# A third activation buffer, a regrouped gate table in DRAM and a later place for two expert pairs in a mixture-of-experts kernel

## The chip, the cores and the metric

The kernel runs on one core of a Trainium2 chip. Its time is the device time of one execution in microseconds (us); three runs gave 2286.55 to 2287.98 us, median 2287.09 us. The profiled execution, from which every row below is taken, was a little longer: 2294.13 us, with a span of 2292.2 us between its first and its last instruction.

The engines are called by short names: PE is the matrix engine, ACT the scalar engine, DVE the vector engine, POOL the GpSimd engine, SP the engine that only issues transfers. A name with a q (SPq, ACTq) means a transfer that the engine issues. Each of the two issuing engines used here, SP and ACT, has a queue of its own (q1 is SP's, q10 is ACT's), and POOL's gathers run on q0. All three are served by the same 16 DMA engines.

## The reference, cut to what matters

Two transformer-like blocks come first; the change does not touch them. Then comes a product-key mixture of experts over 512 tokens, with 16384 experts, each one row of `u_tab` and one row of `v_tab`:

```
def peer(h, wq, subkeys, u_tab, v_tab):          # h: 512 tokens x 1024
    q = (xt @ wq).reshape(T, 8, 2, 128)
    sc = einsum('thpd,hpkd->thpk', q, subkeys)   # 8 heads, two halves, 128 keys each
    vals, ids = top_k(sc, 16)
    cand = vals[:, :, 0, :, None] + vals[:, :, 1, None, :]
    cid  = ids[:, :, 0, :, None] * 128 + ids[:, :, 1, None, :]
    top, pos = top_k(cand, 16)                   # 16 experts per head: 128 per token
    idx = take_along_axis(cid, pos)
    g = softmax(top)
    ...
        u = take(u_tab, ic); a = einsum('chkd,cd->chk', u, xc)
        wgt = gc * gelu(a)
        vv = take(v_tab, ic); out = einsum('chk,chkd->cd', wgt, vv)
```

The result is x plus gate2 times this sum.

## The kernel before, in words

**Two ways through the experts.** The first 128 tokens fetch their chosen rows of u and v with indirect transfers (POOL issues them at L1184, DVE takes the dot products at L1189 and adds the rows at L1203). The other 384 tokens go densely over all 16384 experts, which are cut into 64 pairs of two blocks of 128 experts. A pair needs the activations a = gelu(u h) (128 experts x 2 x 384 tokens), the gate weights g of the same shape (zero where a token did not choose the expert), and the rows of v. Each product is made of three matmuls on a high and a low part.

**What one pair costs on PE.** The activation half is 48 matmuls with 384 columns (`mmps`, L228 to L230, evicted by ACT at L1171), the output half 36 matmuls with 512 columns (`sp`, `tps`, `ob`), which add into six accumulators kept over the whole loop.

**The stages of this part.** After the scores and the choice of experts come the twelve calls of `gates(tb)`, one per block of 32 of the 384 tokens. Each builds the gate weights of its 32 tokens for all 16384 experts in the tile `stg` (ACT evicts it from `sp` at L1352) and writes 2 MB into the DRAM table `gd` (ACT issues this at L1353, right behind the last eviction). Between these calls `act_ahead` makes the activations of pairs 0 to 31 and writes them into `ad` (L1369, ACT's queue). The loop over `order` follows: 32 pairs whose activations are made in the loop (pairs 32 to 63) and 32 whose activations are read from `ad` into the tile `pa` (L1422, SP's queue). Two pairs of the first kind and two of the second take turns; the last four are 62, 63, 30 and 31. Every second pair reads the gate weights of two pairs from `gd` into the tile `pg` (L1427, SP's queue).

**The chain of one pair in the loop.** `vh` is the high part of the rows of v (ACT, L1432) and `vl` the low one (DVE, L1441). DVE multiplies `pa` with `pg` (L1443), ACT rounds the product to `wh` (L1444), DVE makes the rest `wl` (L1445), and the 36 output matmuls follow. `pa` has two buffers, `pg` three; the tile `half` at the end of the kernel shares the buffers of `pa`.

**What sets the order.** A scheduler orders each engine's instructions when the kernel is built, from its own model of time; every engine then runs its list in that order. A tile that is used again waits for the last reader of the buffer. The first tiles of the loop lie in memory that the gates stage used, so they wait for its last transfers as well.

Of the kernel before, what the change touches and what calls it, by code (L numbers as in the profile page):

```python
# [7 lines left out]
F32 = mybir.dt.float32  # L8
# [11 lines left out]
P = 128  # L20
# [117 lines left out]
def body(tc, i, o):  # L138
    nc = tc.nc
    V, A, G, TE, S = nc.vector, nc.scalar, nc.gpsimd, nc.tensor, nc.sync  # L140
    ctx = ExitStack()

    def pool(name, bufs, st=None, **k):
        if "space" not in k:
            k["reuse_waits"] = "tile"
        return (st or ctx).enter_context(tc.tile_pool(name=name, bufs=bufs, **k))
# [11 lines left out]
    dp = pool("dram", 1, space=bass.MemoryType.DRAM)  # L158
# [50 lines left out]
    def load_raw(view, n):  # L209
        r = wraw.tile([P, KD, CW], F32, name="wr", tag="wr")  # L210
        if n == 0:
            r = r.rearrange("p (e k) n -> p e (k n)", e=2)
            S.dma_start(r, view)
            return r
        S.dma_start(r[:, :, :n], view)
        return r
# [10 lines left out]
    def mm3(ps, sh, sl, mh, ml, first, last):  # L227
        TE.matmul(ps, sh, mh, start=first, stop=False)  # L228
        TE.matmul(ps, sh, ml, start=False, stop=False)  # L229
        TE.matmul(ps, sl, mh, start=False, stop=last)  # L230
# [26 lines left out]
    def ada_steps(*mods):  # L257

        ada_run(mods, [load_raw(m.views[m.n][0], CW) for m in mods])
# [880 lines left out]
    TB = 32  # L1140
    ND = T - P
    NTD = ND // P
    NB = ND // TB
# [9 lines left out]
    for t in range(NT):  # L1153
        S.dma_start(xd[t * P:(t + 1) * P, :], x[:, t, :])
    xst.close()
    gd = dp.tile([NB, P, P * TB], F32, name="gd")
    ad = dp.tile([NSP, P, 2 * ND], F32, name="ad")
    gate2 = Rows(aw2[20:24], c2, i["abg2"][5:6])
    idx = gat.tile([P, NH * TK], I32, name="idx")
# [3 lines left out]
    def expert_act(pr, dst, lo_eng=None):  # L1163

        w = load_split(i["u"][pr], CW, lo_eng)
        for e in range(2):
            ps = psm.tile([P, T], F32, name="mmps", tag="mm")
            sl = slice(e * P, (e + 1) * P)
            for k in range(KD):
                mm3(ps[:, :ND], w[0][:, k, sl], w[1][:, k, sl], hT[0][:, k, P:], hT[1][:, k, P:], k == 0, k == KD - 1)  # L1170
            A.activation(dst[:, e, :], ps[:, :ND], AF.Gelu_apprx_tanh)  # L1171
# [40 lines left out]
    def gather_to(goal):  # L1212
        while done[0] < len(work) and done[1] < goal:
            while fetched[0] < len(work) and fetched[1] + work[fetched[0]][0] - done[1] <= NBUF[0]:
                for f in work[fetched[0]][1]:
                    fetch(*f)
                fetched[1] += work[fetched[0]][0]
                fetched[0] += 1
            n, _, fn, args = work[done[0]]
            fn(*args)  # L1220
            done[0] += 1
            done[1] += n
# [105 lines left out]
    def gates(tb):  # L1328

        stg = rw.tile([P, P, TB], F32, name="stg", tag="stg")  # L1330
        for q8 in range(TB // 8):
            t0 = tb * TB + 8 * q8
            bc = lambda a_: a_[:, t0:t0 + 8].unsqueeze(2).to_broadcast([P, 8, P // 2, 2])
            pairs = lambda z: z.rearrange("p t (k s) -> p t k s", s=2)
            oh = [rw.tile([P, 8, P], F16, name="oh" + n, tag="oh" + n) for n in "pohl"]
            p_, o_, qh, ql = oh
            V.tensor_tensor(pairs(p_), pairs(io16), bc(i0T), op=ALU.is_equal)
            V.tensor_tensor(pairs(o_), pairs(io16), bc(i1T), op=ALU.is_equal)
            q = V.tensor_tensor(pairs(qh), pairs(o_), bc(ghT), op=ALU.mult)
            if q8 % 2:  # L1340
                V.tensor_tensor(pairs(ql), pairs(o_), bc(glT2), op=ALU.mult)
            else:
                for n in range(8):
                    A.activation(ql[:, n, :], o_[:, n, :], AF.Copy, scale=glT[:, t0 + n:t0 + n + 1])
            for q4 in range(2):
                ps = pss.tile([P, 4, P], F32, name="sp", tag="sp")
                for n in range(4):
                    j = 4 * q4 + n
                    TE.matmul(ps[:, n, :], qh[:, j, :], p_[:, j, :], start=True, stop=False)
                    TE.matmul(ps[:, n, :], ql[:, j, :], p_[:, j, :], start=False, stop=True)  # L1350
                tl = 8 * q8 + 4 * q4
                A.activation(stg[:, :, tl:tl + 4], ps.rearrange("p t i -> p i t"), AF.Copy, scale=1.0 / 1024)  # L1352
        A.dma_start(gd[tb], stg.rearrange("p i t -> p (i t)"))  # L1353
        with tc.issue_after(q.ins):
            gather_to(max(0, min(tb, 8) - 4) * 3)

# [2 lines left out]
    def act_ahead(n):  # L1359
        for _ in range(n):  # L1360
            pr = ahead[0]
            if pr >= NSP:
                return
            ahead[0] += 1
            if gate2.n < 4:
                ada_steps(gate2)
            a_ = rw.tile([P, 2, ND], F32, name="aout", tag="aout")
            expert_act(pr, a_)
            A.dma_start(ad[pr], a_.rearrange("p a b -> p (a b)"))  # L1369
# [5 lines left out]
    for t in range(NT):  # L1375
        route(t)
        act_ahead(1)
        if t:
            for tb in range(P // TB):
                gates((t - 1) * (P // TB) + tb)  # L1380
                act_ahead(2)
    act_ahead(NSP)
    rt.close()

# [2 lines left out]
    pp = pool("peer", 2)  # L1387
    pa = pool("peeracc", 1)
# [16 lines left out]
    def x_rows(t):  # L1405
        xr = new_rows()
        S.dma_start(xr, xd[t * P:(t + 1) * P, :])
        return xr

    def half_out(t, s_, xr, ps, eng):  # L1410

        sl = slice(s_ * 512, s_ * 512 + 512)
        z = pp.tile([P, 512], F32, name="half", tag="pa")
        V.tensor_mul(z, ps, gate2.out[:, sl])
        eng.tensor_tensor(xr[:, sl], xr[:, sl], z, op=ALU.add)
        S.dma_start(o["out"][t * P:(t + 1) * P, sl], xr[:, sl])

    for step, pr in enumerate(order):
        end = step == len(order) - 1
        a_ = pp.tile([P, 2, ND], F32, name="pa", tag="pa")  # L1420
        if pr < NSP:
            S.dma_start(a_.rearrange("p a b -> p (a b)"), ad[pr])  # L1422
        else:
            expert_act(pr, a_)
        if pr % 2 == 0:
            g4 = pp.tile([P, NB, 4, TB], F32, name="pg", tag="pg", bufs=3)
            S.dma_start(g4.rearrange("p b i t -> p b (i t)"), gd[:, :, 2 * pr * TB:(2 * pr + 4) * TB].rearrange("b p n -> p b n"))  # L1427
        g_ = g4[:, :, 2 * (pr % 2):2 * (pr % 2) + 2, :]
        vr = load_raw(i["v"][2 * pr * P:(2 * pr + 2) * P].rearrange("(e p) d -> p e d", e=2), 0)
        vh = pp.tile([P, 2, D], F32R, name="vh", tag="vh")  # L1430
        vl = pp.tile([P, 2, D], F32R, name="vl", tag="vl")
        A.activation(vh, vr, AF.Copy)  # L1432
        wh = pp.tile([P, 2, ND], F32R, name="wh", tag="wh")
        wl = pp.tile([P, 2, ND], F32R, name="wl", tag="wl")
        pace = []

        def paced(q):
            pace.append(q)
            with tc.issue_after(q.ins):
                gather_to(early + (total - early) * (sum(cost[:step]) + len(pace) / 3 * cost[step]) / fin)  # L1440
        paced(V.tensor_sub(vl, vr, vh.bitcast(F32)))  # L1441
        av = a_.rearrange("p e (b t) -> p e b t", t=TB)
        paced(V.tensor_tensor(av, av, g_.rearrange("p b e t -> p e b t"), op=ALU.mult))  # L1443
        A.activation(wh, a_, AF.Copy)  # L1444
        paced(V.tensor_sub(wl, a_, wh.bitcast(F32)))  # L1445
        if end:
            gather_to(2 * total)
            xrs = [x_rows(t) for t in range(NT)]
            for s_ in range(2):
                half_out(0, s_, xrs[0], acc[:, s_ * 512:s_ * 512 + 512], G)  # L1450
        for t in range(NTD):
            tsl = slice(t * P, (t + 1) * P)
            for s_ in range(2):
                dsl = slice(s_ * 512, s_ * 512 + 512)
                for e in range(2):
                    mm3(sums[2 * t + s_], wh[:, e, tsl], wl[:, e, tsl], vh[:, e, dsl], vl[:, e, dsl], step == 0 and e == 0, end and e == 1)
                if end:
                    half_out(t + 1, s_, xrs[t + 1], sums[2 * t + s_], G if t == 0 and s_ == 0 else V)
# [19 lines left out]
```

## Time and profile before

| | us |
|---|---|
| median of three runs | 2287.09 |
| the profiled execution | 2294.13 |
| its span | 2292.2 |
| blocks 1 and 2 | up to about 1000 |
| scores, choice of experts | about 1000 to 1295 |
| gates: first and last write of `gd` issued | 1302.1, 1478.4 |
| loop over the pairs | about 1487 to 2285 |
| last result issued | 2289.2 |

PE is busy for 96% of the span, DVE for 75%, ACT for 43%, POOL for 26%. The mean over the span hides stages: in most 50-us stretches PE is busy all the time, and there nothing that another engine does moves the end. What can be lost or gained lies where PE's busy time falls short of the stretch, and each place of that kind has a row in the list of waits. A matmul's mean duration in a row is longer than its pitch, because matmuls overlap; the pitch is read from the starts in the timeline. The granted clock (column PEclk, 1.00 is 2.4 GHz, 0.50 is 1.2 GHz) tells whether the matmuls of a stretch ran at full pitch.

### The profile page before, as it was taken

Reading aid. Unit: us, or ns where it says so; the run is one execution under the profiler, and the core shown is the slowest. Engines: PE = TensorE matmul, PEld = TensorE weight load, DVE = VectorE, ACT = ScalarE, POOL = GpSimd, SP = SyncE. Lnnn points to the kernel's source line nnn. Section 1 sums busy time; section 2 is a strip of 40 time slices with the busy share of each in tenths; the row PEclk is TensorE's granted clock in tenths of the full one; section 3 lists DMA queues with packets and bytes.
Section 4 is the critical chain, followed back from the end, with each engine's and each line's share of the span. In section 5 each row is a group of like instructions: output and inputs, shape, how many; then the busy total and the mean of one; then the engine's idle time right before and its main releaser. Section 6 shows DMA issues by size and latency. Waiting matters only on the chain.

```text
span 2292.2 us, 33232 instructions
## 1 busy us (share of the span) xinstructions
PE 2204.9 (96%) x12667; PEld 1901.6 (83%) x12667; DVE 1726.5 (75%) x3497; ACT 984.0 (43%) x1751; POOL 586.5 (26%) x385
## 2 busy tenths in 40 slices
PE   7999999999999989998999999989999999999998
PEld 4777776987789878697899999878888888888887
DVE  6675788488754478658899998687877778778785
ACT  3335565444433353544334677723333323333331
POOL 1231100210101441010000002155545545435451
PEclk9989999999999899999999999999999999999999
DMA  7531120145432124024345468899989999999993
GB/s 292 207 137 49 38 74 19 65 160 185 158 112 90 38 75 158 19 103 146 127 153 204 180 266 329 310 376 342 333 324 353 336 336 347 333 337 359 332 340 138
DMA packets 151823, 474.38 MB, mean 207 GB/s; under 512 B 14320, under 2 KB 66416, under 8 KB 128624
## 3 DMA queue, kind: packets, MB, share of 16 engines
q1 hardware_dynamic: 108464, 300.28, 36.9%
q0 software_dynamic: 36864, 134.23, 15.6%
q10 hardware_dynamic: 6336, 37.75, 4.2%
q8 instruction: 99, 1.62, 0.3%
q14 instruction: 60, 0.49, 0.1%
HBM read 429.76 MB, written 41.94 MB: 206 GB/s over the span
## 4 chain that ended last, share of the span: by engine, by line
PE 82%; DVE 7%; DMA 5%; ACT 2%; issue 2%; POOL 1%; SPq 0%; ACTq 0%; DVEq 0%; POOLq 0%
PE mmps L228 14%; PE mmps L230 14%; PE mmps L229 14%; PE sp L228 4%; PE sp L229 4%; PE sp L230 4%; PE tps L228 3%; PE sp L490 3%; PE tps L229 2%; PE tps L230 2%; PE tps L514 2%; PE ob L738 2%; DVE adacc L269 2%; DMA pa<-ad 1%; DMA wr<-in_aw_dram 1%
## 5 line engine op out<-in xcount | busy, mean ns | idle before, releaser
L228 PE MATMUL mmps<-hTh,whi 128*128 128x384 f32 (+1 forms) x1624 | 588.8, 364 | 6.1 <-ACT pa L1171 2.5
L229 PE MATMUL mmps<-hTl,whi 128*128 128x384 f32 (+1 forms) x1624 | 584.0, 360 | 1.7 <-DVE hTl L346 1.7
L230 PE MATMUL mmps<-hTh,wlo 128*128 128x384 f32 (+1 forms) x1624 | 582.6, 359 | 2.2 <-DVE wlo L224 2.2
L1184 POOL DMA_INDIRECT rows<-in_un_dram,idx x128 | 211.3, 1651 | 593.7 <-DVE rows L1189 333.6
L228 PEld LDWEIGHTS mmps<-hTh,whi 128*128 128x128 f32 x1624 | 306.6, 189 | 37.8 <-ACT pa L1171 3.7
L230 PEld LDWEIGHTS mmps<-hTh,wlo 128*128 128x128 f32 x1624 | 306.6, 189 | 30.1 <-DVE wlo L224 3.0
L229 PEld LDWEIGHTS mmps<-hTl,whi 128*128 128x128 f32 x1624 | 307.0, 189 | 29.0 <-DVE hTl L346 3.3
L223 ACT ACTIVATE whi<-wr 128x2048 fp32r<-128x2048 f32 x121 | 230.2, 1903 | 154.6 <-PE mmps L229 97.2
L224 DVE TENSOR_TENSOR wlo<-wr,whi 128x2048 fp32r<-128x2048 f32 x111 | 253.1, 2280 | 32.9 <-ACT whi L223 32.3
L1184 POOL DMA_INDIRECT rows<-in_v_dram,idx x128 | 198.4, 1550 | 211.4 <-DVE acc L1203 171.1
L1441 DVE TENSOR_TENSOR vl<-wr,vh 128x2048 fp32r<-128x2048 f32 x64 | 146.5, 2289 | 119.2 <-ACT vh L1432 106.7
L1432 ACT ACTIVATE vh<-wr 128x2048 fp32r<-128x2048 f32 x64 | 122.4, 1914 | 264.4 <-PE ob L230 223.1
L1203 DVE SCALAR_TENSOR_TENSOR acc<-rows,dots,acc 128x1024 f32<-128x1024 f32 x127 | 162.6, 1280 | 1.8 <-DMA rows<-in_v_dram,idx 0.2
L269 DVE SCALAR_TENSOR_TENSOR adacc<-wr,c_c,adacc 128x256 f32<-128x256 f32 x308 | 161.3, 541 | 3.2
L1189 DVE SCALAR_TENSOR_TENSOR rows<-rows,hn 128x1024 f32<-128x1024 f32 x128 | 153.2, 1218 | 10.8 <-DMA rows<-in_un_dram,idx 9.8
L228 PE MATMUL sp<-vh,wh 128*128 128x512 f32 x384 | 145.6, 396 | 13.2 <-ACT wh L1444 13.2
L229 PE MATMUL sp<-vl,wh 128*128 128x512 f32 x384 | 148.7, 395 | 1.5 <-DVE vl L1441 1.5
L230 PE MATMUL sp<-vh,wl 128*128 128x512 f32 x384 | 136.7, 391 | 0.4 <-DVE wl L1445 0.4
L1444 ACT ACTIVATE wh<-pa 128x768 fp32r<-128x768 f32 x64 | 53.2, 842 | 160.6 <-DVE pa L1443 90.8
L228 PE MATMUL mmps<-whi,hTh 128*128 128x256 f32 x336 | 106.6, 318 | 4.2 <-ACT whi L223 2.9
L229 PE MATMUL mmps<-wlo,hTh 128*128 128x256 f32 x336 | 103.9, 310 | 0.6 <-DVE wlo L224 0.6
L230 PE MATMUL mmps<-whi,hTl 128*128 128x256 f32 x336 | 102.5, 311 | 1.1 <-DVE hTl L346 1.1
(1087 smaller groups left out, 4351.0 us busy)
## 6 DMA issues: line engine op xcount, KB each, us to landing
wr<-in_u_dram SPq DMA_DIRECT2D x64, 1024.0 KB
wr<-in_v_dram SPq DMA_DIRECT2D x64, 1024.0 KB
wr<-in_aw_dram SPq DMA_DIRECT2D x48, 1024.0 KB
gd<-stg ACTq DMA_DIRECT2D x12, 2048.0 KB
pg<-gd SPq DMA_DIRECT2D x32, 768.0 KB
wr<-in_dilw_dram SPq DMA_DIRECT2D x16, 1024.0 KB
ad<-aout ACTq DMA_DIRECT2D x32, 384.0 KB
pa<-ad SPq DMA_DIRECT2D x32, 384.0 KB
```

What stands on the lines that cost most here:

```text
L223: A.activation(hi[:, :, :n], r[:, :, :n], AF.Copy)
L224: (lo_eng or V).tensor_tensor(lo[:, :, :n], r[:, :, :n], hi[:, :, :n].bitcast(F32), op=ALU.subtract)
L228: TE.matmul(ps, sh, mh, start=first, stop=False)
L229: TE.matmul(ps, sh, ml, start=False, stop=False)
L230: TE.matmul(ps, sl, mh, start=False, stop=last)
L269: V.scalar_tensor_tensor(acc, r[:, k, :], m.ccol[:, k:k + 1], acc, op0=ALU.mult, op1=ALU.add)
L490: TE.matmul(sp[j], q, k, start=False, stop=True, skip_group_check=True)
L1184: G.indirect_dma_start(out=r, out_offset=None, in_=table, in_offset=bass.IndirectOffsetOnAxis(ap=ix, axis=0))
L1189: V.scalar_tensor_tensor(r, r, 1.0, hn, op0=ALU.mult, op1=ALU.mult, accum_out=dots[:, n:n + 1])
L1203: V.scalar_tensor_tensor(acc, r, dots[:, n:n + 1], acc, op0=ALU.mult, op1=ALU.add)
L1432: A.activation(vh, vr, AF.Copy)
L1441: paced(V.tensor_sub(vl, vr, vh.bitcast(F32)))
```

## The change

It has four edits. The DRAM table `gd` is laid out as [128, 32, 12, 128] in place of [12, 128, 4096]: its second index is a group of four first keys, that is of two pairs, so that what one read takes is contiguous for each partition. The two pairs that `act_ahead` makes less in the first two rounds of the gates are left to the call `act_ahead(NSP)` behind the last gates. The tile `pa` gets a third buffer, `half` with it, and `pg` gives one up.

```
-    gd = dp.tile([NB, P, P * TB], F32, name="gd")
+    gd = dp.tile([P, P // 4, NB, 4 * TB], F32, name="gd")
...
-        A.dma_start(gd[tb], stg.rearrange("p i t -> p (i t)"))
+        A.dma_start(gd[:, :, tb, :], stg.rearrange("p (g i) t -> p g (i t)", i=4))
...
-                act_ahead(2)
+                act_ahead(1 if t == 1 and tb < 2 else 2)
     act_ahead(NSP)
...
-        z = pp.tile([P, 512], F32, name="half", tag="pa")
+        z = pp.tile([P, 512], F32, name="half", tag="pa", bufs=3)
...
-        a_ = pp.tile([P, 2, ND], F32, name="pa", tag="pa")
+        a_ = pp.tile([P, 2, ND], F32, name="pa", tag="pa", bufs=3)
...
-            g4 = pp.tile([P, NB, 4, TB], F32, name="pg", tag="pg", bufs=3)
-            S.dma_start(g4.rearrange("p b i t -> p b (i t)"), gd[:, :, 2 * pr * TB:(2 * pr + 4) * TB].rearrange("b p n -> p b n"))
+            g4 = pp.tile([P, NB, 4, TB], F32, name="pg", tag="pg", bufs=2)
+            S.dma_start(g4.rearrange("p b i t -> p (b i t)"), gd[:, pr // 2].rearrange("p b n -> p (b n)"))
```

**ACT in the gates stage.** The names: `gd<-stg` is the write of gate weights, `ad<-aout` that of activations made ahead. Before:

```order
L1369 DMA ad<-aout 128x768
L1353 DMA gd<-stg 128x4096
L1171 ACTIVATE aout<-mmps 128x384
L1352 ACTIVATE stg<-sp 128x128x4 x3
L1344 ACTIVATE ohl<-oho,glT 128x128 x8
```

After, at the same place:

```order
L1369 DMA ad<-aout 128x768
L1353 DMA gd<-stg 4096x1x128
L1171 ACTIVATE aout<-mmps 128x384
L1352 ACTIVATE stg<-sp 128x128x4 x3
L1344 ACTIVATE ohl<-oho,glT 128x128 x8
```

Nothing moved here; only the write's shape differs, 4096 runs of 128 numbers (512 bytes) where there were 128 runs of 4096 numbers (16 KB). On PE, ACT, DVE and SP the whole list up to the first instructions of the loop holds the same operations in the same order, and all 32 writes of `ad` stand ahead of the last write of `gd`, before and after.

**SP at the start of the loop.** These are the transfers that stand in its queue one behind the other. Before:

```order
L213 DMA wr<-in_v_dram 128x2x1024 x2
L1427 DMA pg<-gd 128x12x128 x3
L213 DMA wr<-in_v_dram 128x2x1024
L215 DMA wr<-in_u_dram 128x2048
L1422 DMA pa<-ad 128x768
L1427 DMA pg<-gd 128x12x128
L1422 DMA pa<-ad 128x768
```

After:

```order
L213 DMA wr<-in_v_dram 128x2x1024 x2
L1427 DMA pg<-gd 128x1536 x2
L213 DMA wr<-in_v_dram 128x2x1024
L1422 DMA pa<-ad 128x768
L215 DMA wr<-in_u_dram 128x2048
L1422 DMA pa<-ad 128x768
L1427 DMA pg<-gd 128x1536
```

Two reads of `pg` stand ahead of the rows of v and not three, the first `pa` stands ahead of the load of u, and a read is 128 runs of 6 KB where it was 1536 runs of 512 bytes.

**PE where the last activations are made.** `mmps_20511` is the second block of pair 63, `wh_20423` and `wh_20542` are the rounded products of pairs 62 and 63. Before:

```order
L229 MATMUL mmps_20511<-hTl_9756,whi_20481 128x384
L230 MATMUL mmps_20511<-hTh_9755,wlo_20482 128x384
L228 MATMUL sp_14928<-vh_20539,wh_20542 128x512
L229 MATMUL sp_14928<-vl_20540,wh_20542 128x512
L228 MATMUL sp_14929<-vh_20539,wh_20542 128x512
```

After:

```order
L229 MATMUL mmps_20511<-hTl_9756,whi_20481 128x384
L230 MATMUL mmps_20511<-hTh_9755,wlo_20482 128x384
L228 MATMUL sp_14928<-vh_20420,wh_20423 128x512
L229 MATMUL sp_14928<-vl_20421,wh_20423 128x512
L228 MATMUL sp_14929<-vh_20420,wh_20423 128x512
```

Before, the output matmuls of pair 63 stand right behind its own last activation; after, the 36 output matmuls of pair 62 stand between the two.

## Rows read from the trace of the kernel before

**Rows 1.** Windows: length, busy us of PE, PEld, DVE, ACT, POOL (instructions), clock, DMA share, GB/s.

```profile
1500.00:1550.00 50.00, 48.60 (x231) 42.01 (x230) 39.34 (x48) 15.92 (x13) 25.01 (x16) 0.99 1.04 391
...
1650.00:1700.00 50.00, 48.26 (x232) 41.76 (x231) 38.90 (x48) 16.16 (x14) 28.32 (x17) 1.00 0.94 341
1700.00:1750.00 50.00, 50.00 (x239) 43.51 (x238) 37.64 (x45) 15.93 (x13) 26.29 (x16) 1.00 0.93 331
```

**Rows 2.** Waits of PE from 1300 to the end: total us, times, longest.

```profile
PE sp L228 <- ACT wh L1444: 13.2, 4, 8.1
```

**Rows 3.** Timeline from the last gate write to the first product, ACT and DVE.

```profile
1478.40 0.33 ACTq L1353 DMA_DIRECT2D gd<-stg  x1
...
1488.97 2.29 DVE L1441 TENSOR_TENSOR vl<-wr,vh 128x2048 fp32r<-128x2048 f32 x1 [12.34 <-DMA gd<-stg]
...
1494.12 0.96 DVE L1443 TENSOR_TENSOR pa<-pa,pg 128x768 f32<-128x768 f32 x1 [0.57 <-DMA pg<-gd]
```

**Rows 4.** Timeline of the loop's end, PE and DVE.

```profile
2255.45 0.34 PE L230 MATMUL mmps<-hTh,wlo 128*128 128x384 f32 x1
...
2257.72 0.95 DVE L1443 TENSOR_TENSOR pa<-pa,pg 128x768 f32<-128x768 f32 x1
...
2259.60 0.80 PE L228 MATMUL sp<-vh,wh 128*128 128x512 f32 x1 [3.82 <-ACT wh L1444]
2260.20 0.63 PE L229 MATMUL sp<-vl,wh 128*128 128x512 f32 x1
2260.62 0.63 PE L228 MATMUL sp<-vh,wh 128*128 128x512 f32 x1
```

**Rows 5.** Matmuls at full clock just before, and windows of 5 us around that gap.

```profile
2252.68 0.39 PE L228 MATMUL ob<-vh,wh 128*128 128x512 f32 x1
2252.91 0.39 PE L229 MATMUL ob<-vl,wh 128*128 128x512 f32 x1
...
2255.00:2260.00 5.00, 1.18 (x6) 0.87 (x5) 4.49 (x4) 2.27 (x4) 0.00 (x0) 0.84 0.00 0
2260.00:2265.00 5.00, 5.00 (x13) 3.85 (x13) 4.29 (x5) 0.28 (x1) 0.00 (x0) 0.50 0.55 184
```

**Rows 6.** Waits of PE between 1500 and 2250.

```profile
PE sp L229 <- DVE vl L1441: 1.5, 1, 1.5
PE mmps L230 <- DVE wlo L224: 1.3, 1, 1.3
PE sp L228 <- ACT wh L1444: 1.2, 2, 1.0
PE mmps L228 <- ACT pa L1171: 0.9, 3, 0.5
```

**Rows 7.** DMA queues from 1302 to 1480, then from 1489 to 1500: packets, MB, share.

```profile
q10 hardware_dynamic: 3744, 28.97, 40.8%
...
q1 hardware_dynamic: 4675, 2.44, 88.2%
```

**Rows 8.** Windows: the gates stage as a whole.

```profile
1302.00:1478.00 176.00, 173.55 (x1447) 164.72 (x1445) 158.07 (x233) 134.42 (x303) 18.91 (x14) 1.00 0.78 297
```

**Rows 9.** Instructions by tile: duration ns min/median/max, first and last start.

```profile
L1353 ACTq DMA_DIRECT2D gd<-stg x12: 326/326/327, 1302.1 to 1478.4; - x12
L1369 ACTq DMA_DIRECT2D ad<-aout x15: 326/326/327, 1310.7 to 1459.6; - x15
L1422 SPq DMA_DIRECT2D pa<-ad x32: 320/338/7836, 1501.6 to 2260.8; - x32
```

**Rows 10.** Timeline of SP where the first gate weights are read.

```profile
1488.92 0.37 SPq L1427 DMA_DIRECT2D pg<-gd  x1
1489.46 0.61 SPq L1427 DMA_DIRECT2D pg<-gd  x1
1490.16 2.73 SPq L1427 DMA_DIRECT2D pg<-gd  x1
```

**Rows 11.** What ended DVE's and ACT's idle time before work on `pa`: us, times.

```profile
  DMA pa<-ad: 23.2, 8
```

## The prediction

> **What bounds the kernel now.** I read the busy shares first, then windows of 50 us, then PE's list of waits, and last the timeline at each place where a wait of PE stands. The windows tell where to look. From 1700 on PE is busy 50.00 of 50 us per window, at full clock, up to the last 50 us: only PE's own work counts there. Between 1500 and 1700 every window falls short, the first by 1.4 and the last by 1.74 us, the four together by 5.1 us [rows 1]. The largest wait by far is that of an output matmul for `wh`, 13.2 us in four times, the longest 8.1 us [rows 2]. It has two homes. One is the passage from the gates to the loop: the last write of `gd` is issued at 1478.40, DVE resumes at 1488.97 when it has landed, and the product at L1443 starts at 1494.12, when the first `pg` has landed [rows 3]. The other is the loop's end: PE makes the last activation at 2255.45, waits 3.82 us for the chain eviction, product, `wh` of that same pair, and runs on from 2259.60 [rows 4].
>
> **The end: -6.4 us.** The order puts the 36 output matmuls of pair 62 between the last activation and the first matmul that needs its `wh`. At full clock such a matmul takes 0.23 us (starts 2252.68 and 2252.91 [rows 5]), so 36 of them cover 8.2 us; the chain to be covered is 2255.45 to 2259.60, 4.15 us [rows 4]. The gap of 3.82 us goes. With it goes what follows it: PE's granted clock is 1.00 before the gap and 0.50 in the 5 us from 2260 (2.4 and 1.2 GHz), with 13 matmuls there [rows 5], which start 0.42 us apart (2260.20, 2260.62 [rows 4]) instead of 0.23: 13 x 0.2 = 2.6 us. What is late next is PE itself. If a load of `pa` for pairs 30 or 31 came late, the same gap would only move; the third buffer lets that load start earlier, so I take the whole 6.4 us, with 0 as the other end.
>
> **Inside the loop: -4 us.** The waits of PE from 1500 to 2250 add up to 4.9 us, of which `wlo` has 1.3 [rows 6]. A third `pa` lets the next pair's activations be evicted and the next `ad` read be issued before the product of the pair before last is used up, and a `pg` read of 8 runs per DMA engine in place of 96 lets what stands behind it in SP's queue start sooner. I take 4 of the 5.1 us missing in the windows [rows 1]; more than 5.1 there is not to be had. Nothing or a loss is possible, since `pg` with two buffers is asked for later and the order is a new one (third rival).
>
> **The gates' last write and first read: +1.9 us.** Prices per megabyte come from the queues. Long runs (8 KB on average): 40.8% of 16 engines for 178 us moved 28.97 MB, 40 engine-us per MB. Runs of 512 bytes: 88.2% of 16 engines for 11 us moved 2.44 MB, 64 engine-us per MB [rows 7]. A write of 2.1 MB thus goes from 5.3 to 8.3 us, +3.1; a read of 0.79 MB from 3.1 to 2.0 us, -1.2. Both lie on the passage's chain one behind the other [rows 3], so +1.9. The ends: -1.2, if a write of 512-byte runs drains as the long one does, and +3.1, if the read gains nothing because its landing is mostly latency. No row shows a write of short runs.
>
> **The other eleven writes: +3 us.** As transfers they lie beside PE's work: PE is busy 173.55 of 176 us in this stage and the DMA engines 0.78 [rows 8]; 12 x 3.1 = 37 us more lift that to 0.99, full but not over. The doubtful part is ACT, which issues them. A write now holds ACT for 0.33 us [rows 9]. After, it has 4096/16 = 256 runs per DMA engine. The nearest rows are SP's three reads in a row, 96 runs per engine each: the first held SP for 0.37 us, the second (192 in all) for 0.61, the third (288) for 2.73 [rows 10]; the three together, 3.97 us, are where 288 leads and 1.1 us where 192 does. In between 256 gives 3.0 us, 2.7 more than now, 12 times: 32 us of ACT's time. ACT has 176 - 134.42 = 41.6 us to spare there [rows 8], so by the sum it is hidden behind PE; but the hold always stands ahead of an eviction, and PE has only two buffers of `mmps` to go on with. I take a tenth of it, 3 us. The ends: -2.4, all of PE's idle time there [rows 8], and +49: a hold as long as the longest of the trace, 7.84 us [rows 9], makes 12 x 7.5 = 90 us against 41.6.
>
> The Trainium skill, Perfetto Trace Analysis, section "DMA Instruction — HWDGE (DVE, Sync)", says that the issuing sequencer stays occupied, with the descriptor generator locked, until all descriptors of its transfer have been generated, and that the descriptor buffer can fill. SP's third read agrees, with its 2.73 us [rows 10]; no row here shows ACT held so. By that rule the sum is the first rival's rather than mine.
>
> **The moved pairs: 0.** The pairs that `act_ahead` leaves out in the first rounds are made at the same place as before: the order up to the loop is unchanged and all writes of `ad` still stand ahead of the last of `gd` (the last now starts at 1459.6 [rows 9]). Their matmuls therefore cover nothing of the passage. So this edit doesn't do what it says, and I count it at nothing.
>
> **The sum.** -6.4 - 4 + 1.9 + 3 = -5.5 us. From the profiled execution, 2294.1, that is 2288.6; this execution stands 7.0 us above the median of the runs, so the forecast is 2287.1 - 5.5 = 2281.6 us. About 0.2%, 4.6 us, is what a measurement of this kernel can tell from no change.
>
> **Rivals.**
> *ACT held until its queue drains (slower).* The new writes share the DMA engines with loads and gathers, so their runs drain more slowly than SP's reads did. Halfway between 3.0 and the longest hold, 7.84 us [rows 9], is 5.4 us: 12 x 5.1 = 61 us, 20 more than ACT has to spare, and PE waits for evictions in the gates stage. Sum -6.4 - 4 + 1.9 + 20 = +11.5: 2299 us. It decides from a hold of 4.5 us on (12 x 4.2 = 50 = 41.6 + 8.5 of gains). For it: SP's 2.73 and 7.84 us. Against it: two reads, with 192 of the 256 runs per engine, were taken in within 1.1 us [rows 10]. Chance 0.26.
>
> *The loop keeps its waits (no change).* The DMA engines are at 1.04 and 0.94 in the windows that fall short [rows 1]; if it is their load and not the buffers that makes `pa`, `vl` and `wlo` late, nothing is gained there: -6.4 + 0 + 1.9 + 3 = -1.5: 2285.6 us. For it: the longest single waits there are for `vl` and `wlo` [rows 6], which no edit touches. Chance 0.24.
>
> *A new wait at the loop's start (slower).* The order now has pair 33's product behind pair 0's on DVE, and pair 0's waits for its `ad` read. DVE and ACT have waited 23.2 us for such reads in eight times [rows 11], and one was held 7.84 us at issue [rows 9]. If it hits here, PE stands 7.8 us and pays the 2.6 us of half clock once more: 10.4 - 6.4 + 1.9 + 3 = +8.9: 2296 us. Against it: the same read now stands ahead of the load of u and behind one `pg` fewer. Chance 0.08.
>
> **How the numbers follow.** The forecast has 0.42; its own range is 2277 to 2284, from how much of the loop's 5.1 us goes and whether the gates lose 0 to 6. Faster 0.42, within 0.2% 0.24, slower 0.26 + 0.08 = 0.34. The range for 8 in 10 runs from 2276, a little below the case in which nothing is lost in the gates, to 2310; above it lies the part of the first rival with holds over 6.3 us (12 x 6 - 41.6 - 8.5 = +22), about one in ten.
>
> **What would show it.** Right at the end: no wait for `wh` near 2255, and no window at half clock there. Right in the loop: PE busy 50 of 50 between 1550 and 1700. Passage: from the issue of the last `gd` write to DVE's first product 17 to 18 us (now 15.7). Gates: issues of L1353 of about 3 us, and the stage from the first to the last of them no more than 180 us. The forecast is wrong if those issues last over 4.5 us, or if PE's busy time in that stage falls more than 8 us short; then the whole loop stands later by as much.

## The result and the profile after

The changed kernel takes 2304.11 us (median of six runs, 2298.61 to 2309.88) against 2287.82 us before in the same six rounds: the ratio is 1.0072, 95% interval 1.0055 to 1.0089. It is slower, by 16 us, where 5.5 us faster was forecast. The profiled execution has a span of 2302.9 us (2292.2 before), so of the two profiled executions it is the slower by 10.7 us.

Three stages share these 10.7 us, and a fourth has no part in the change: the first write of `gd` came 5.0 us earlier in this execution (1297.1 and 1302.1), although the lists of instructions up to there are the same; the other profiles below put it anywhere from 1294 to 1302 us. From the first to the last write of `gd` the stage takes 198.8 us, where it took 176.3: +22.5. From the last write to the first product it takes 21.0 us, 15.7 before: +5.3. From there to the end it is 786.0 us, 798.0 before: -12.0. So -5.0 + 22.5 + 5.3 - 12.0 = 10.8, the 10.7 but for rounding.

Where the stage lost its time is read from windows (columns as in [rows 1]). The first line answers to [rows 8]; the others are two stretches of it and the loop:

```profile
1297.00:1496.00 199.00, 181.75 (x1447) 169.36 (x1445) 157.49 (x233) 133.84 (x303) 20.93 (x14) 0.96 0.81 260
...
1405.00:1410.00 5.00, 5.00 (x46) 4.59 (x44) 5.00 (x6) 0.88 (x2) 0.00 (x0) 1.00 0.96 321
1410.00:1415.00 5.00, 0.23 (x2) 0.10 (x1) 0.09 (x1) 0.00 (x0) 0.00 (x0) 0.91 1.07 390
1415.00:1420.00 5.00, 1.30 (x10) 1.30 (x10) 0.00 (x0) 2.33 (x7) 0.00 (x0) 0.50 0.98 310
1420.00:1425.00 5.00, 5.00 (x19) 4.94 (x17) 3.52 (x5) 4.36 (x9) 0.00 (x0) 0.56 0.04 15
...
1440.00:1445.00 5.00, 2.33 (x19) 2.03 (x18) 0.00 (x0) 0.20 (x1) 0.00 (x0) 0.98 1.09 382
1445.00:1450.00 5.00, 4.14 (x21) 2.66 (x21) 1.77 (x3) 5.00 (x15) 0.00 (x0) 0.50 0.36 129
...
1550.00:1600.00 50.00, 50.00 (x249) 44.87 (x248) 37.46 (x44) 18.60 (x16) 20.88 (x14) 1.00 0.91 340
1650.00:1700.00 50.00, 50.00 (x240) 43.64 (x239) 39.29 (x49) 16.42 (x14) 27.97 (x18) 1.00 0.90 336
```

PE executes the same matmuls (1447 records in either stage), but stands still for 17.3 us, where it stood for 2.5, and its busy time is 8.2 us longer. There are two bad places, near 1412 and near 1443. In each PE and ACT fall idle together, and when PE resumes its granted clock is 0.50, so the same matmuls take longer. In the loop the windows that fell short before [rows 1] are now full from 1550 on, but for 0.23 us in the one from 1600; the first, from 1500, holds the later passage.

What PE waited for in the gates stage, and in the loop:

```profile
PE sp L1349 <- ACT stg L1352: 13.5, 7, 8.5
...
PE mmps L228 <- ACT pa L1171: 0.7, 3, 0.2
PE sp L230 <- DVE wl L1445: 0.5, 1, 0.5
PE mmps L230 <- DVE wlo L224: 0.3, 1, 0.3
```

The first line is of the gates stage alone, where this wait was 0.8 us, once, before; the other three are all waits of PE from 1520 to the end, 1.5 us in place of the 4.9 us of [rows 6] and the 3.8 us of [rows 4].

Why ACT was late is in the issues, by tile (columns as in [rows 9], which the first two lines answer to):

```profile
L1353 ACTq DMA_DIRECT2D gd<-stg x12: 520/521/587, 1297.1 to 1495.8; - x12
L1369 ACTq DMA_DIRECT2D ad<-aout x16: 322/2582/11658, 1292.5 to 1474.5; - x16
...
L1427 SPq DMA_DIRECT2D pg<-gd x32: 319/320/372, 1512.5 to 2226.8; - x32
...
L1422 SPq DMA_DIRECT2D pa<-ad x32: 319/425/713, 1513.9 to 2263.3; - x32
```

The write of short runs itself holds ACT for 0.52 us only. It is the next transfer on ACT's queue that is held, a write of `ad`, whose 128 runs were issued in 0.33 us before and now take up to 11.66 us. On SP's queue, where the reads became 12 times fewer runs, the longest hold of a `pa` read fell from 7.84 to 0.71 us. ACT's timeline at the worst place:

```profile
1402.96 0.52 ACTq L1353 DMA_DIRECT2D gd<-stg  x1
1403.58 1.92 ACT L223 ACTIVATE whi<-wr 128x2048 fp32r<-128x2048 f32 x1 [0.65 <-ACT stg L1352]
1405.40 0.47 ACT L1171 ACTIVATE aout<-mmps 128x384 f32<-128x384 f32 x1
1405.91 11.66 ACTq L1369 DMA_DIRECT2D ad<-aout  x1
1417.67 0.49 ACT L1171 ACTIVATE aout<-mmps 128x384 f32<-128x384 f32 x1 [11.79 <-issue]
1418.05 1.08 ACT L1352 ACTIVATE stg<-sp 128x512 f32<-128x512 f32 x2
```

PE's next gate matmul needs the eviction that stands behind the held transfer; it starts at 1418.70 after 8.46 us. SP, meanwhile, issues:

```profile
1408.31 0.33 SPq L215 DMA_DIRECT2D wr<-in_u_dram  x1
```

SP's load is issued in 0.33 us in the middle of ACT's hold, and SP's loads in five more of ACT's nine holds are issued in 0.33 to 0.38 us. So it is the transfer ahead in the same queue that holds, not a generator shared by both.

The passage, SP, DVE and ACT (the lines answer to [rows 3] and [rows 10]):

```profile
1495.85 0.52 ACTq L1353 DMA_DIRECT2D gd<-stg  x1
...
1512.53 0.81 SPq L1427 DMA_DIRECT2D pg<-gd  x2
...
1516.89 0.96 DVE L1443 TENSOR_TENSOR pa<-pa,pg 128x768 f32<-128x768 f32 x1 [13.19 <-DMA pg<-gd]
```

From the last write's issue to the first read's it takes 16.7 us (10.5 before, 1478.40 to 1488.92), from there to the product 4.4 us (5.2 before).

And the end of the loop on PE, where [rows 4] had the gap:

```profile
2264.77 0.34 PE L230 MATMUL mmps<-hTh,wlo 128*128 128x384 f32 x1
2264.95 0.39 PE L228 MATMUL sp<-vh,wh 128*128 128x512 f32 x1
2265.18 0.40 PE L229 MATMUL sp<-vl,wh 128*128 128x512 f32 x1
2265.41 0.40 PE L228 MATMUL sp<-vh,wh 128*128 128x512 f32 x1
```

There is no gap, and the output matmuls start 0.23 us apart, at full clock.

### The profile page after: what moved, and what is told of

Same layout as the page of the kernel before. It is cut to its first block, busy times and chain, and to the rows that moved or that the text cites. A ratio compares the mean times of both kernels' runs of the same rounds, so it can differ in the third digit from the quotient of the medians.

```text
span 2302.9 us, 33235 instructions
## 1 busy us (share of the span) xinstructions
PE 2202.7 (96%) x12667; PEld 1900.4 (83%) x12667; DVE 1727.7 (75%) x3497; ACT 982.9 (43%) x1751; POOL 579.0 (25%) x385
## 5 line engine op out<-in xcount | busy, mean ns | idle before, releaser
L224 DVE TENSOR_TENSOR wlo<-wr,whi 128x2048 fp32r<-128x2048 f32 x111 | 253.2, 2281 | 43.9 <-ACT whi L223 43.3
L1184 POOL DMA_INDIRECT rows<-in_v_dram,idx x128 | 192.1, 1501 | 224.3 <-DVE acc L1203 179.4
```

Of the source, the lines that this page charges most:

```text
L224: (lo_eng or V).tensor_tensor(lo[:, :, :n], r[:, :, :n], hi[:, :, :n].bitcast(F32), op=ALU.subtract)
L1184: G.indirect_dma_start(out=r, out_offset=None, in_=table, in_offset=bass.IndirectOffsetOnAxis(ap=ix, axis=0))
```

## The experiments

The theory after the result: the write of short runs costs what was lost, through ACT's queue, and the order that follows from three `pa` buffers and two `pg` buffers gains what was gained. The two parts can be run alone, because they separate cleanly. With the old table the three buffers give the changed kernel's instruction lists; with the old buffers the new table gives the lists of before. The moved pairs were not run alone: without that edit the lists of all engines are the same as with it, names apart.

**The buffers alone.**

```
 before, with
-        a_ = pp.tile([P, 2, ND], F32, name="pa", tag="pa")
+        a_ = pp.tile([P, 2, ND], F32, name="pa", tag="pa", bufs=3)
-            g4 = pp.tile([P, NB, 4, TB], F32, name="pg", tag="pg", bufs=3)
+            g4 = pp.tile([P, NB, 4, TB], F32, name="pg", tag="pg", bufs=2)
 ("half" with bufs=3 too)
```

> Three buffers of pa and two of pg, the table gd as before: the instruction lists of the changed kernel, with 16 KB writes and 512-byte reads. Theory: the write of short runs is what costs (the stage from the first to the last write of gd 176 us again, and 15.7 us from the last write to the first product), and the new order of the loop gains 12 us by itself (6.4 at its end, the rest inside): 2275 to 2280 us, 8 to 12 below before. Rival: the loop's gain comes from the contiguous reads of pg; then only the end's 6.4 us are left, 2281 us, and PE has waits of about 5 us between 1500 and 1700 again.

Measured: 2280.72 us, ratio 0.9969 (0.9957 to 0.9982): faster than both kernels. It lies 0.7 us above the theory's range and on the rival's 2281 us, so the time does not decide between the two; the stages and the waits do. The stage takes 176.3 us, the passage 17.2 us (1.5 more than the theory had), the rest 788.4 us, 9.6 us less than before. The stage as a window, and PE's waits from 1500 on:

```profile
1297.00:1474.00 177.00, 173.86 (x1449) 165.05 (x1448) 158.45 (x234) 135.18 (x304) 19.57 (x14) 1.00 0.79 296
...
PE sp L228 <- ACT wh L1444: 0.9, 1, 0.9
PE mmps L228 <- ACT pa L1171: 0.7, 3, 0.2
PE mmps L230 <- DVE wlo L224: 0.6, 3, 0.3
```

The theory's first half holds. Of the loop's 12.0 us the order and the buffers give 9.6; the other 2.4 would be the contiguous reads', as far as one execution of each kernel can tell. The rival, that the reads bring everything but the end's 6.4 us, falls: of the waits between 1500 and 1700 some 0.2 us are left with reads of 512 bytes too. SP's queue still has its holds here: a load of u behind a `pg` read is held for 7.22 us (from 1514.55), which the changed kernel, with its contiguous reads, no longer shows.

**The table alone.**

```
 before, with
-    gd = dp.tile([NB, P, P * TB], F32, name="gd")
+    gd = dp.tile([P, P // 4, NB, 4 * TB], F32, name="gd")
 and the write at L1353 and the read at L1427 as in the changed kernel
```

> The new table gd alone: the instruction lists of before, with writes of 512-byte runs and contiguous reads. Theory: the gates stage grows by 22 us and the passage by 5 us as in the changed kernel, and the end keeps its gap of 3.8 us: 2310 to 2316 us. Rival: the loss in the gates comes from the new order or the moved pairs; then this stays within 2285 to 2293 us.

Measured: 2310.99 us, ratio 1.0095 (1.0079 to 1.0112). The stage takes 198.1 us, the passage 19.0, the rest 794.2 us (3.8 less than before, where only the reads differ). So the passage grew by 3.3 us and not by 5; the end keeps its wait of 3.8 us. The holds come at the same places with nearly the same lengths:

```profile
L1369 ACTq DMA_DIRECT2D ad<-aout x16: 321/2215/11908, 1295.4 to 1477.0; - x16
```

With every instruction in the place that it has in the kernel before, the loss in the gates belongs to the table alone. The two parts add up: -7.8 and +22.5 us in the medians make +14.7, against +16.3 for both.

**The writes of `ad` on another queue.**

```
 changed kernel, with
-            A.dma_start(ad[pr], a_.rearrange("p a b -> p (a b)"))
+            G.dma_start(ad[pr], a_.rearrange("p a b -> p (a b)"))
```

> The changed kernel with the writes of ad issued by POOL and not by ACT, so that no transfer stands behind a write of gd on ACT's queue. Theory: ACT loses its time only where its next transfer has to wait for the write of gd; without it the stage is 176 to 180 us again and the time 2284 to 2288 us. Rival: the short runs fill the DMA engines and make loads late; then the stage stays near 198 us and the time at 2300 us or more.

Measured: 2289.68 us, ratio 1.0005 (0.9992 to 1.0018). Two groups of rows of this run: the issues of `ad`, now POOL's, and the stage:

```profile
L1369 POOL DMA_DIRECT2D ad<-aout x16: 539/542/603, 1295.9 to 1462.8; - x16
```

```profile
1300.00:1476.00 176.00, 173.77 (x1447) 164.81 (x1446) 157.67 (x233) 134.51 (x303) 31.78 (x30) 1.00 0.89 293
```

With nothing behind the short-run write on ACT's queue the stage is back at 175.7 us, PE's clock at 1.00, while the DMA engines are busier than before (0.89 against 0.78 [rows 8]). So the load on the DMA engines is not what stopped PE. The time is 1.7 us above what was expected: the scheduler ordered this kernel anew, and its passage (20.2 us) and loop (791.9 us) are longer than those of the buffers alone. For the same reason this run does not change the queue alone; the run with half as many runs, further down, leaves the order as it was.

**No gathers during the gates.**

```
 changed kernel, with
-            gather_to(max(0, min(tb, 8) - 4) * 3)
+            gather_to(0)
```

> The changed kernel without row gathers during the gates (all of them are then made in the loop). Theory: the two longest holds of ACT (11.7 and 8.4 us) are those in which the runs of gd share the DMA engines with gathered rows; without these every hold is 4 us at most and the stage 183 to 190 us: 2289 to 2297 us. Rival: the holds come from the 257 descriptors per engine alone; then the stage stays near 198 us and the time above 2300 us.

Measured: 2298.01 us, ratio 1.0045 (1.0027 to 1.0063). The holds that are left are of 4 us at most, seven above 2 us, and they cost nothing:

```profile
L1369 ACTq DMA_DIRECT2D ad<-aout x16: 320/326/3962, 1293.7 to 1464.4; - x16
```

```profile
1298.00:1474.00 176.00, 174.34 (x1448) 164.59 (x1446) 145.53 (x209) 133.26 (x304) 2.74 (x3) 1.00 0.82 258
```

The stage is 175.9 us, shorter than theory and rival had it: a hold of 4 us hides behind PE's work, and it is the two long ones that made most of the 22 us. The gain did not reach the time, because the rest took 805.2 us, 19 more than in the changed kernel: the row gathers moved into the loop, the order there is another one, and the idle gap with half clock at the loop's end is back. This run is no clean proof that gathers make the holds long, since the order of the gates changed a little as well and the write of `ad` near the worst place now stands 7 us behind that of `gd`, not 3.

**Half as many runs.**

```
 changed kernel, with
-    gd = dp.tile([P, P // 4, NB, 4 * TB], F32, name="gd")
+    gd = dp.tile([P, P // 8, NB, 8 * TB], F32, name="gd")
 the write in groups of eight first keys, the read of four of the eight
```

> The changed kernel with the table in groups of eight first keys: writes of 2048 runs of 1 KB (129 descriptors per DMA engine with the last one, in place of 257), reads of 1536 runs of 512 bytes as before. Theory: what holds ACT's next transfer is the number of descriptors that still stand in its queue, and up to about 190 were taken without a hold; then every write of ad is issued in under 1 us, the stage from the first to the last write of gd takes 176 to 178 us, and the time is that of the run with the old table, 2278 to 2284 us. Rival: the hold lasts as long as the bytes of gd need beside gathers and loads; then the two long holds keep 4 to 8 us each and the time is 2287 us or more.

Measured: 2282.74 us, ratio 0.9979 (0.9965 to 0.9993).

```profile
L1369 ACTq DMA_DIRECT2D ad<-aout x16: 321/326/4177, 1291.2 to 1453.3; - x16
```

All engines' lists are those of the changed kernel, so in the gates only the runs of the write differ, and the stage is back at 176.3 us. The time is as the theory said, but not every hold is gone: the four transfers behind the busiest places were held for 4.2, 2.9, 1.3 and 3.1 us. Nor does the number of descriptors still to go set the length: a transfer issued with 110 per DMA engine left was held for 0.75 us, one with 93 left for 2.92 us. How fast the queue drains has a part in it, as the rival said, only with lengths that PE does not notice.

**The pairs really behind the gates.**

```
 buffers alone, with act_ahead(1 if t == 1 and tb < 2 else 2) and
-    act_ahead(NSP)
+    with tc.issue_after(glast[0].ins):    # the last matmul of the gates
+        act_ahead(NSP)
```

> The old table with three buffers of pa, and the last two pairs of act_ahead tied behind the last matmul of the gates, so that the scheduler cannot draw them forward. Theory: 96 activation matmuls of 0.17 us, 16.6 us, then cover the passage from the last write of gd to the first product: PE's gap of 8 us and its half clock go, but the last gates, which ACT's evictions pace, lose PE work to put between them; 2272 to 2279 us, below the run without the tie (2280.7). Rival: the gates are paced by ACT, so what PE gains in the passage it loses ahead of it: 2278 to 2284 us, no difference.

Measured: 2280.36 us, ratio 0.9974 (0.9957 to 0.9990), the same as without the tie. The wait for `wh` at the passage goes (9.6 us in the buffers alone):

```profile
PE sp L1351 <- DVE ohh L1341: 4.8, 4, 3.3
PE sp L1351 <- ACT stg L1354: 3.7, 5, 2.1
PE sp L1351 <- DVE ohp L1339: 2.0, 2, 1.8
PE sp L228 <- ACT wh L1447: 1.3, 1, 1.3
```

In its place PE waits in the last gates for DVE and ACT (the first three lines; line numbers are two to three higher here), with fewer activation matmuls to put between. The rival holds in its time, since the idle time only moves; what paces the last gates is DVE (6.8 us of these waits) more than ACT (3.7 us).

## Why the prediction was wrong

**The step that failed** is the term for the other writes of `gd`, +3 us, where the runs showed +22.5 us. I put the hold at the write itself, about 3 us each, and charged a tenth of the twelve. But the write is issued in 0.52 us, and it is the next transfer of the same queue that is held. That moves the question from how many writes there are to what stands behind each: nine of the writes of `ad` were held, with lengths from 2.4 to 11.7 us, 46 us in all, and ACT had 41.6 us to spare [rows 8]. A sum over the stage could not have told the outcome. In the run without gathers the holds add up to 24 us, in the one with half the runs to 11, and both cost nothing; what counts is the length of a single hold against what PE has in front of it. Holds of 4 us cost nothing; the two of 11.7 and 8.4 us made most of the 22.5 us, of which 14.8 are idle time of PE and the rest, some 8, slower matmuls, where the granted clock was 0.50 after the two stops.

The first rival (ACT held, +20 us in the gates, 2299 us) had the right engine and the right stage, but that its 20 lies near the 22.5 is luck: it came from holds of 5.4 us at all twelve writes, 61 us against 41.6. By that sum the 46 us that were measured would have cost some 4 us.

The trace of the kernel before already had the case. The longest hold, 7.84 us [rows 9], which I used only as a length, fell on a read of 128 runs, and what stood ahead of it in SP's queue was a read of 1536 short ones, issued in 0.38 us:

```profile
1655.89 0.38 SPq L1427 DMA_DIRECT2D pg<-gd  x1
1657.91 7.84 SPq L1422 DMA_DIRECT2D pa<-ad  x1
```

**How a hold gets long** is read from the DMA queues in the changed kernel. The lines give packets, MB and share of the 16 engines, first from 1317 to 1324, around a hold of 3.9 us, where ACT's queue has the DMA engines almost to itself; then from 1405 to 1417, in the hold of 11.7 us, where a load of u and gathered rows run at the same time:

```profile
q10 hardware_dynamic: 3276, 1.67, 86.3%
q1 hardware_dynamic: 22, 0.18, 13.2%
...
q10 hardware_dynamic: 3076, 1.57, 43.3%
q1 hardware_dynamic: 230, 1.62, 34.4%
q0 software_dynamic: 288, 1.05, 25.9%
```

In either stretch some 3100 to 3300 short runs go out, but in the second they share with 230 and 288 packets of some 7 and 4 KB and need 12 us in place of 7. I had the share of the stage as a whole (0.78 [rows 8]) and the longest hold of the trace (7.84 us [rows 9]), but took the interpolation of three reads that ran with little beside them for the likeliest. In the 4 us after the write's issue the queues of SP and POOL moved 0.86 and 0.24 MB, and of ACT's not one packet went out:

```profile
q1 hardware_dynamic: 117, 0.86, 65.6%
q0 software_dynamic: 63, 0.24, 18.9%
```

So the hold of 11.7 us begins with all of the write's descriptors still to go, the one of 3.9 us with 224 of 257 per DMA engine. That the neighbours lengthen the hold is argued from these counts; no run took only them away.

**The passage**, +1.9 forecast, +5.3 measured. The read's gain was right in size (0.8 us, 1.2 forecast). The last write took 16.7 us to the first read's issue, 6.2 more and not 3.1: it was issued 7 us behind the write before it, of which 53 descriptors per DMA engine had still to go (none before, at 6.5 us). The order alone adds nothing to this part: with the old table and the new order it is 10.6 us, with the new table and the old order 14.5, and 16.7 only with both. Until the last write had landed, POOL's queue moved 720 packets of gathered rows in the changed kernel, 432 with the table alone and 393 before; that these make the difference between 14.5 and 16.7 is not shown.

**The end and the loop**, -10.4 forecast, -12.0 measured: right in mechanism and size. The gap at the end is gone with its half clock, and PE's waits inside the loop fell from 4.9 to 1.5 us; the buffers alone give 9.6 of it. The rival that the DMA load keeps these waits falls with that run, and the new wait at the loop's start did not come. (Of the windows from 1700 on, which I called full in the kernel before, the one from 1750 held 49.77 us; nothing hangs on it.)

**The moved pairs**, 0: right by the order, and the run that ties them behind the gates shows that the edit would bring nothing if it did what it says.

**The rule set beside the sum**, from the Trainium skill (Perfetto Trace Analysis, section "DMA Instruction — HWDGE (DVE, Sync)": the sequencer is occupied and the generator locked until all descriptors are made), warned of the right danger. An issuing engine is indeed held in the trace, and the holds end with 49 to 95 descriptors per DMA engine still to land, which agrees with a buffer that fills; the trace differs in the place: ACT was released after 0.52 us with all 257 descriptors per DMA engine still to land, the next transfer of ACT's own queue had to wait, and SP's issues were not delayed.

## What to carry to other kernels

Before a transfer's layout is changed for the reader's sake, look at what its issuing engine does next: a write of many short runs is posted at once, and the bill comes at the next transfer in the same queue, together with all of that engine's work behind it. A hold costs nothing up to the work that the bound engine has in front of it (4 us here), and beyond that it costs the rest and, where the granted clock falls, slower matmuls besides. So the longest hold decides and not the sum. Where a change has parts that a scheduler lets one separate, run the parts: here one gained 0.31% and the other lost 0.95%.

## What was not expected of the hardware

Twelve writes with 257 descriptors per DMA engine (4112 packets of ACT's queue on 16 engines) were each taken in within 0.52 to 0.59 us, more than the three reads of [rows 10] had let one expect, while a transfer of 9 descriptors per engine behind one of them was held for up to 11.66 us. In the changed kernel 49 to 95 descriptors per engine of the two transfers together were still outstanding at the end of a hold, by the packets that had landed; where fewer than 35 were left at the issue there was no hold. Up to 53 left brought none either in the changed kernel's last write of `gd`, up to 52 in the run without gathers and up to 59 in the one with half the runs. What the limit is made of, no run here shows.
